# Pair operands in steps, early products, modulation and norm statistics on another engine, in a two-block transformer kernel

## The chip, the cores and the metric

The kernel runs on one core of a Trainium2 chip, as one program. The metric is the device time of one execution in microseconds; of several runs the median is taken. In the profile the engines are PE (TensorE, matrix products), DVE (VectorE), ACT (ScalarE), POOL (GpSimd) and SP (SyncE, which issues most transfers).

## What is computed

Two blocks of two layers each, on 1024 tokens of 1024 features, in float32 (products are done as three partial products of a high and a low part).

```python
# first block, per layer
h = x * (1 + scale) + shift              # "modulation": scale, shift, gate from c @ w_mod
u = h @ w_in                             # also for 256 context tokens
y = concat(rwkv(u), attention(u), neighbourhood(u)) * silu(gates)
x = layer_norm(ALPHA * x + gate * (y @ w_out), ln_g, ln_b)
...
# second block
h = layer_norm(x, ln_in_g, ln_in_b)
for l in range(2):
    fq, fk, fv, flog, sq, sk, sv, cq, ckv, krot, mq, gate = split(h @ w_in[l])
    fox = causal_softmax(fq, fk, fv, 1/8, cumsum(log_sigmoid(flog + b)))
    sb  = stick_breaking(sq, sk, sv, 1/8)
    mla = causal_softmax(up(cq), up(ckv) + rope(krot), ..., 96 ** -0.5)
    mem = softmax(mq @ mk / 8) @ mv      # 256 memory tokens
    h = layer_norm(ALPHA * h + (concat(fox, sb, mla, mem) * silu(gate)) @ w_out[l], ln_g[l], ln_b[l])
```

## The kernel before, in words

The input of a layer is kept transposed in SBUF as a high and a low half, `hthi` and `htlo`, in groups of tokens `GROUPS = ((0, 256), (256, 512), (768, 512))`: the context, and two halves of the 1024 tokens. From the second block on there is no group 0. A projection of 128 columns for one group is 24 matmuls (`proj_part`, `proj_b`): eight chunks of features, three partial products each. `open_layer` makes room for the next layer's halves and loads and splits its first 128 columns of weights.

**Between layers.** `out_proj` works on tiles of 128 tokens: 48 matmuls into two tiles `po`; in the first block a multiply by the gate (`r`, L1713); `x = ALPHA x + r` (L1715); `layer_norm`, in the last layer of the first block a second one with the second block's first weights (`post`); the store; and `put_ht`, which turns the tile (`xtp`, L109), in the first block's first layer modulates it (`hmod`, L409, eight instructions of 128 columns per tile on DVE with two per-partition operands), and splits it into `hthi` (ACT, L127) and `htlo` (DVE, L128). `layer_norm` takes its statistics with `bn_stats` on DVE (L183, L184), the inverse root by ACT and DVE, then 384 columns on ACT, POOL and DVE and 640 on DVE. `out_proj` is not in a fixed order: the framework orders each engine's instructions by a simulated time line. The next layer's first projection (`conv(..., 9)` in `project`, or `bcols` of `ckv` in `block2_layer`) follows in PSUM tiles `pj`, whose pool is opened after `out_proj` has closed its own.

**Attention of the second block.** Within `self.ordered()` PE executes in the order of the program text; the other engines are ordered by the framework. Two streams of steps are woven by `seqs`: `soft_heads` (two pairs of MLA heads, two pairs of fox heads) at rate 48 and `other_heads` (two pairs of stick-breaking heads, two pairs of memory heads) at rate 32. The stream whose count of steps, each of 1/rate, is lowest goes next. A pair begins with `pump(todo, 0)`, which executes the transposes and products that the pair before still owes, then makes its operands: `queries2` (load, scaled copy on ACT, copy to the other half by POOL, low part on DVE, per head: `bform`, L1204 and L1208), `keys2` (load, two casts on ACT, two low parts on DVE: `aform`, L1194 to L1197), `values2` (a load). `spare` gives the room of the raw load: for the soft stream the tag "P" (two buffers, also the room of the weights), for the other stream the one buffer "sa" of the stick-breaking weights. Then come two yields (`gap`: at a stream's first pair with `GAP` = 3 fillers each), and the pair's units: eight tiles of queries, 12 steps in a causal pair, four steps in a memory pair.

A step issues scores for one group (`weigh`), then what is due of the groups before (`turn`: transposes of the weights `PTp` and their copies `PT`; after every four blocks `fill`, one filler; `blend`: the product with the values, `Yp`). The filler generator gives pieces of the layer's other projections, six matmuls each (`proj2`), then the split of the output weights. `need` draws fillers until the named projections are done.

```python
seqs((self.soft_heads(ap, proj), 48), (self.other_heads(ap, proj, l), 32))
...
Q = self.queries2(pool, "a", 6 + p, scale)
K = self.keys2(pool, "a", 4 + p)
V = self.values2(pool, "a", 4 + p)
...
self.need(proj, ("g", 4 + p))
yield from self.gap(p == 0)
yield from self.causal(pool, todo, "a", 4 + p, ...)
```

The functions that the change touches:

Of the kernel before, what the change touches and what calls it, by code (L numbers as in the profile page):

```python
# [71 lines left out]
class Kern:  # L72
    def __init__(self, tc, A, out):
# [12 lines left out]
        self.ptp = None  # L86

# [89 lines left out]
    def layer_norm(self, pool, src, dst, g, b):  # L177

        nc = self.nc
        st = self.tl(pool, [128, 2, 6], F32, "lnst", 2)  # L180
        mv = self.tl(pool, [128, 5], F32, "lnmv", 2)
        for i in range(2):
            nc.vector.bn_stats(st[:, i, :], src[:, i * 512:(i + 1) * 512])  # L183
        nc.vector.bn_aggr(mv[:, 0:2], st)  # L184
        self.rstd(mv[:, 2:3], mv[:, 1:2], 1.0, 1e-5, mv[:, 3:4], mv[:, 4:5])
# [206 lines left out]
    def put_ht(self, sp, pp, ht, t, xt, mc):  # L392
# [5 lines left out]
        for half in range(2):  # L398
# [85 lines left out]
    def project(self, l, ht, full, first, fp, sd, att):  # L484
# [4 lines left out]
        with ExitStack() as es:  # L489
# [109 lines left out]
    def conv(self, sp, pp, ht, hi, lo, j, bufs=5):  # L599
# [5 lines left out]
        for g, (s, n) in enumerate(GROUPS):  # L605
            ps = yield from self.psteps(pp, ht, g, hi, lo)
# [592 lines left out]
    def bform(self, B, L, raw, scale, side=(0, 1)):  # L1199

        nc = self.nc
        for h in range(2):
# [476 lines left out]
    def out_proj(self, es, wo, tiles, t0, l, g, b, gated, mc, xi, xo, post=None, side=None):  # L1679
# [4 lines left out]
        sp = self.pool(es, "op", side=side)  # L1684
        pp = self.pool(es, "opp", space=PSUM, side="right")
# [11 lines left out]
        for t in tiles:  # L1697
# [6 lines left out]
            for c in range(2):  # L1704
# [55 lines left out]
    def block2_layer(self, l, i):  # L1760
# [8 lines left out]
        with ExitStack() as es:  # L1769
# [4 lines left out]
            with ExitStack() as s3:  # L1774
                mp = self.pool(s3, "mla", side=far)
                up = self.pool(s3, "up2", space=PSUM)
# [7 lines left out]
                self.bcols(pj, ht, *first, 0, 128, ckv)  # L1784
                for hi, lo, m, dst in self.ahead(fp, st, W, ((1, 36, kf), (2, 128, cq[:, 0]), (3, 128, cq[:, 1]))):
                    self.bcols(pj, ht, hi, lo, 0, m, dst)
# [61 lines left out]
    def bcols(self, pp, ht, hi, lo, c0, m, dst):  # L1848
        for g in (1, 2):
            s, n = GROUPS[g]  # L1850
            ps = self.proj_b(pp, ht, g, hi, lo, c0, m)
# [186 lines left out]
    def keys2(self, pool, tag, j):  # L2038
        K = self.tl(pool, [128, 2, NL], F32R, tag + "K")
        raw = self.spare(pool, tag)  # L2040
        self.load(raw, self.RK[j])
# [19 lines left out]
    def soft_heads(self, pool, proj):  # L2061
# [6 lines left out]
        kf = self.spare(pool, "a")  # L2068
# [5 lines left out]
        for p in range(2):  # L2074
            self.pump(todo, 0)
            Q = self.queries2(pool, "a", 6 + p, scale)
            K = self.keys2(pool, "a", 4 + p)
            V = self.values2(pool, "a", 4 + p)
            raw = self.spare(pool, "a")
            self.load(raw, self.QP)  # L2080
# [8 lines left out]
            yield from self.gap(p == 0)  # L2089
            yield from self.causal(pool, todo, "a", 4 + p, lambda h, t, tk, n: self.qk_scores(  # L2090
                Q, h, K[:, h], tk, self.span(n), t, extra=(qr[:, h], krs)), V)
        for p in range(2):
            self.need(proj, ("q", p), ("k", p), ("v", p), ("g", p))
            self.pump(todo, 0)
            Q = self.queries2(pool, "a", p, 0.125)
            K = self.keys2(pool, "a", p)
# [4 lines left out]
            yield  # L2101
            yield
# [185 lines left out]
```

## Time and profile before

| | us |
|---|---|
| median of three runs | 3996.33 |
| the three runs | 3978.35, 3996.33, 4007.02 |
| the profiled execution | 3984.52 |
| its span, first to last instruction | 3982.7 |
| PE busy in it | 3608.7 |
| DVE, ACT, POOL busy | 2639.5, 1713.5, 1166.4 |

Mean granted clock of TensorE: 0.955 of full speed; it has two levels, 1.2 and 2.4 GHz. In a row of the timeline stand the start, the duration, the engine, the line, the operation, the tiles (out<-in), the shapes, the count, and in brackets the idle time of the engine before it and what ended it. PE's rows overlap, as matmuls are pipelined. Stages by their start in the span: first block's first layer 0, its output projection 1183, second layer 1331, its output projection 2367, second block's projections 2497, attention 2655, output projection 3161, second layer's projections 3262, attention 3385, output projection 3885.

### The profile page before, as it was taken

How to read it: one execution, taken by the hardware profiler on the slowest of the kernel's cores; microseconds unless marked ns; L12 is line 12 of the kernel's file. 1: busy time of each engine (PE TensorE's matmuls, PEld its weight loads, DVE VectorE, ACT ScalarE, POOL GpSimd, SP SyncE). 2: the span in 40 equal slices, each digit the busy share in tenths (PEclk: the TensorE clock that was granted, in tenths of full speed). 3: DMA queues.
4: the chain of work that ended last, by engine and by line, in shares of the span. 5: the costliest groups of instructions: out<-in, count | busy, mean ns of one | idle time of the engine just before them, and what ended most of it. 6: DMA issues, size and time to landing. Idle time of an engine off the chain costs nothing. (4 is left out here: it accounts for less than half of the span.)

```text
span 3982.7 us, 67431 instructions
## 1 busy us (share of the span) xinstructions
PE 3608.7 (91%) x25828; PEld 2696.0 (68%) x25828; DVE 2639.5 (66%) x4778; ACT 1713.5 (43%) x3352; POOL 1166.4 (29%) x1175
## 2 busy tenths in 40 slices
PE   7999998989979899898999888999889899888988
PEld 5767776666537777676666546677667677666767
DVE  4546886677878745886686769556665554676654
ACT  3236553444442335553444342345454423555451
POOL 2200012556662210001566653031111311221232
PEclk8999998999989999898999999999999999999999
DMA  7437864242533227875243522341222332322233
GB/s 252 162 116 185 200 164 144 87 137 87 177 106 106 83 77 182 185 186 167 84 136 97 173 90 90 127 137 64 80 83 83 130 122 95 103 83 86 87 98 130
DMA packets 509843, 495.74 MB, mean 124 GB/s; under 512 B 296360, under 2 KB 412616, under 8 KB 505168
## 3 DMA queue, kind: packets, MB, share of 16 engines
q1 hardware_dynamic: 469264, 455.76, 38.2%
q10 hardware_dynamic: 40256, 35.66, 3.0%
q8 instruction: 204, 3.34, 0.4%
q14 instruction: 119, 0.97, 0.1%
HBM read 323.81 MB, written 167.49 MB: 123 GB/s over the span
## 5 line engine op out<-in xcount | busy, mean ns | idle before, releaser
L106 PE MATMUL pj<-hthi,hhi 128*128 128x512 f32 (+2 forms) x2120 | 857.2, 404 | 22.9 <-DVE stg L712 13.1
L106 PE MATMUL pj<-hthi,hlo 128*128 128x512 f32 (+2 forms) x2120 | 805.4, 380 | 0.0
L106 PE MATMUL pj<-htlo,hhi 128*128 128x512 f32 (+2 forms) x2120 | 804.5, 379 | 0.4 <-DVE htlo L128 0.4
L106 PEld LDWEIGHTS pj<-hthi,hhi 128*128 128x128 f32 (+1 forms) x2120 | 407.3, 192 | 126.8 <-issue 23.6
L106 PEld LDWEIGHTS pj<-hthi,hlo 128*128 128x128 f32 (+1 forms) x2120 | 405.5, 191 | 79.6 <-DVE hlo L128 0.4
L106 PEld LDWEIGHTS pj<-htlo,hhi 128*128 128x128 f32 (+1 forms) x2120 | 408.6, 193 | 61.0 <-DVE htlo L128 1.6
L1554 POOL TENSOR_TENSOR acc<-acc,gP 128x512 f32<-128x512 f32 (+1 forms) x240 | 306.4, 1291 | 140.0 <-ACT gP L1548 123.5
L1548 ACT ACTIVATE gP<-T 128x512 f32<-128x512 f32 (+1 forms) x292 | 166.9, 582 | 167.3 <-PE T L106 153.8
L1460 DVE TENSOR_REDUCE gmx<-S 128x1 f32<-128x512 f32 (+1 forms) x372 | 202.1, 554 | 47.1 <-PE S L106 44.9
L106 PE MATMUL po<-who,yh 128*128 128x512 f32 x544 | 214.6, 395 | 11.0 <-ACT yh L1668 8.5
L127 ACT CAST hhi<-hraw 128x1024 fp32r<-128x1024 f32 x118 | 123.8, 1049 | 231.2 <-PE pj L106 194.3
L106 PE MATMUL po<-wlo,yh 128*128 128x512 f32 x544 | 214.3, 394 | 0.0
L106 PE MATMUL po<-who,yl 128*128 128x512 f32 x544 | 212.1, 392 | 0.7 <-POOL yl L1669 0.7
L106 PE MATMUL S<-K,B 128*128 128x512 f32 (+2 forms) x448 | 168.9, 381 | 46.3 <-DVE gmx L1460 34.7
L106 PE MATMUL Y<-gP,V 128*64 128x512 f32 (+1 forms) x776 | 203.2, 603 | 3.0 <-DVE ys L1567 2.9
L128 DVE TENSOR_TENSOR hlo<-hraw,hhi 128x1024 fp32r<-128x1024 f32 x84 | 102.8, 1223 | 128.3 <-ACT hhi L127 127.4
L106 PE MATMUL T<-B,K 128*128 128x512 f32 (+1 forms) x368 | 167.9, 457 | 10.5 <-ACT gP L1548 9.2
L1189 POOL TENSOR_SCALAR RL<-rl 128x128 f32<-128x128 f32 (+1 forms) x80 | 34.6, 434 | 469.6 <-DVE rl L1306 417.8
L106 PEld LDWEIGHTS S<-K,B 128*128 128x128 f32 x448 | 86.6, 193 | 122.3 <-DVE gmx L1460 73.7
L128 POOL TENSOR_TENSOR hlo<-hraw,hhi 128x1024 fp32r<-128x1024 f32 x34 | 87.0, 2559 | 256.4 <-ACT hhi L127 249.6
L106 PE MATMUL S<-KL,L 128*128 128x512 f32 (+2 forms) x448 | 153.7, 353 | 2.0 <-ACT KL L1380 2.0
L106 PE MATMUL T<-L,KL 128*128 128x512 f32 (+1 forms) x368 | 144.7, 394 | 0.0
(420 smaller groups left out, 8037.3 us busy)
## 6 DMA issues: line engine op xcount, KB each, us to landing
hraw<-in_w_in_dram SPq DMA_DIRECT2D x110, 512.0 KB
T<-d_PRE SPq DMA_DIRECT2D x40, 768.0 KB
mw<-in_w_mod_dram SPq DMA_DIRECT2D x24, 1024.0 KB
RKK<-d_U SPq DMA_DIRECT2D x80, 288.0 KB
yl<-d_YT ACTq DMA_DIRECT2D x34, 512.0 KB
d_G<-stg SPq DMA_DIRECT2D x64, 256.0 KB
woraw<-in_w_out_dram SPq DMA_DIRECT2D x32, 512.0 KB
d_PRE<-T SPq DMA_DIRECT2D x40, 384.0 KB
```

What stands on the lines that cost most here:

```text
L106: self.nc.tensor.matmul(out, lhsT=lhsT, rhs=rhs, start=start, stop=stop, skip_group_check=True)
L127: self.nc.scalar.copy(hi, src)
L128: self.lo_engine.tensor_tensor(out=lo, in0=src, in1=hi.bitcast(F32), op=ALU.subtract)
L1189: self.nc.gpsimd.tensor_scalar(out=out, in0=in_, scalar1=1.0, scalar2=0.0, op0=ALU.mult, op1=ALU.add)
L1460: nc.vector.tensor_reduce(out=m, in_=S[:, 0:w], op=ALU.max, axis=AX.X, negate=True)
L1548: nc.scalar.activation(P, T, AF.Exp)
L1554: eng.tensor_tensor(out=acc[h][:, cs], in0=acc[h][:, cs], in1=P, op=ALU.add)
```

## The change

Five things are changed.

1. Operands of a pair (second block). `gap` becomes `step`, one yield, with three fillers before it if it is told that it is the stream's first. `spare` also issues the load; query and key loads of a pair are issued together, in "P" (soft stream) or in two of the three buffers "sc" (other stream). `queries2` yields after each head, and there is a step after the loads and one after the keys: four per pair; in a memory pair three.
2. Early products. In `out_proj`, after the matmuls of the last tile and before its norm, the first 128 columns of the next layer are multiplied for groups 0 and 1, where they exist, into PSUM tiles of their own (`early`). `conv` and `bcols` take them instead of making them.
3. Modulation in `put_ht` goes from DVE to ACT (the first block's first layer, 80 instructions; 16 more for the memory tokens).
4. Sums. In the norm `post`, for all but the last two tiles, mean and variance come from two ACT passes with `accum_out` instead of `bn_stats`.
5. The pool `up2` is opened after the first `bcols`.

```diff
-    def layer_norm(self, pool, src, dst, g, b):
+    def layer_norm(self, pool, src, dst, g, b, sums=False):
...
+        if sums:
+            junk = self.tl(pool, [128, D], BF16, "lnj")
+            nc.scalar.activation(junk, src, AF.Identity, scale=-1.0 / D, accum_out=mv[:, 5:6])
+            nc.scalar.activation(junk, src, AF.Square, bias=mv[:, 5:6], accum_out=mv[:, 1:2])
+            nc.vector.tensor_scalar(out=mv[:, 0:1], in0=mv[:, 5:6], scalar1=-1.0, scalar2=None, op0=ALU.mult)
...
-                    nc.vector.tensor_scalar(out=h[:, j, :], in0=ps[:, j, :], scalar1=mc[:, v, 8 + k:9 + k],
-                                            scalar2=mc[:, v, k:k + 1], op0=ALU.mult, op1=ALU.add)
+                    nc.scalar.activation(h[:, j, :], ps[:, j, :], AF.Identity, scale=mc[:, v, 8 + k:9 + k], bias=mc[:, v, k:k + 1])
...
                 dd = self.drain(self.conv(kq, pp, ht, *first, 9))
+                self.early[0].close()
...
-            ps = yield from self.psteps(pp, ht, g, hi, lo)
+            ps = self.early[1].pop(g, None)
+            if ps is None:
+                ps = yield from self.psteps(pp, ht, g, hi, lo)
...
+        groups = [g for g in (0, 1) if nht and g in nht]
+        if nht:
+            ep = self.pool(self.early[0], "early", space=PSUM, side="right" if 0 in nht else "left")
...
+            if t == tiles[-1]:
+                for g in groups:
+                    n = GROUPS[g][1]
+                    ps = self.early[1][g] = self.tl(ep, [128, 512], F32, f"early{g}")[:, :n]
+                    self.proj_part(ps, nht, g, *self.nht[2], 0, 8)
             self.layer_norm(sp, x, x, gr, br)
             if post:
-                self.layer_norm(sp, x, x, pg, pb)
+                self.layer_norm(sp, x, x, pg, pb, sums=t < tiles[-2])
...
-    def gap(self, first):
-
-        for _ in range(2):
-            for _ in range(GAP if first else 0):
-                next(self.filler, None)
-            yield
+    def step(self, first=False):
+
+        for _ in range(GAP if first else 0):
+            next(self.filler, None)
+        yield
...
-    def spare(self, pool, tag):
-
-        return self.tl(pool, [128, NL], F32, "P", 2) if tag == "a" else self.tl(pool, [128, NL], F32, "sa")
-
-    def queries2(self, pool, tag, j, scale):
+    def spare(self, pool, tag, src):
+
+        raw = self.tl(pool, [128, NL], F32, *(("P", 2) if tag == "a" else ("sc", 3)))
+        self.load(raw, src)
+        return raw
+
+    def queries2(self, pool, tag, raw, scale, first=False):
...
-        raw = self.spare(pool, tag)
-        self.load(raw, self.RQ[j])
-        self.bform(B, L, raw, scale)
+        for h in range(2):
+            self.bform(B, L, raw, scale, heads=(h,))
+            yield from self.step(first)
         return B, L
...
         for p in range(2):
             self.pump(todo, 0)
-            Q = self.queries2(pool, "a", 6 + p, scale)
-            K = self.keys2(pool, "a", 4 + p)
+            rq, rk = self.spare(pool, "a", self.RQ[6 + p]), self.spare(pool, "a", self.RK[4 + p])
             V = self.values2(pool, "a", 4 + p)
-            raw = self.spare(pool, "a")
-            self.load(raw, self.QP)
+            yield from self.step(p == 0)
+            Q = yield from self.queries2(pool, "a", rq, scale, p == 0)
+            raw = self.spare(pool, "a", self.QP)
+            K = self.keys2(pool, "a", rk)
+            yield from self.step()
...
             self.need(proj, ("g", 4 + p))
-            yield from self.gap(p == 0)
             yield from self.causal(pool, todo, "a", 4 + p, lambda h, t, tk, n: self.qk_scores(
...
-            Q = self.queries2(pool, "b", 2 + p, 0.125)
-            K = self.keys2(pool, "b", 2 + p)
+            rq, rk = self.spare(pool, "b", self.RQ[2 + p]), self.spare(pool, "b", self.RK[2 + p])
             V = self.values2(pool, "b", 2 + p)
-            yield from self.gap(p == 0)
+            yield from self.step(p == 0)
+            Q = yield from self.queries2(pool, "b", rq, 0.125, p == 0)
+            K = self.keys2(pool, "b", rk)
+            yield from self.step()
```

The fox pairs (soft stream) and the memory pairs (other stream) are changed alike, without fillers in their steps.

## Rows read from the trace of the kernel before

**Rows 1.** The page, first part: busy time, share of the span, instructions.

```profile
PE 3608.7 (91%) x25828; PEld 2696.0 (68%) x25828; DVE 2639.5 (66%) x4778; ACT 1713.5 (43%) x3352; POOL 1166.4 (29%) x1175
```

**Rows 2.** Windows, stages: length, then busy (instructions) PE, PEld, DVE, ACT, POOL; clock, DMA.

```profile
1183.00:1331.00 148.00, 123.49 (x559) 99.74 (x559) 117.92 (x245) 34.04 (x61) 34.90 (x32) 0.93 0.35 110
...
2367.00:2497.00 130.00, 106.64 (x468) 84.96 (x467) 108.23 (x228) 34.73 (x73) 43.15 (x28) 0.91 0.28 93
...
2655.00:3161.00 506.00, 441.57 (x2901) 340.80 (x2899) 327.82 (x488) 268.44 (x480) 121.56 (x88) 0.95 0.27 88
3161.00:3262.00 101.00, 99.10 (x465) 82.40 (x466) 58.76 (x121) 23.52 (x46) 25.07 (x16) 1.00 0.43 144
```

**Rows 3.** Windows, twelve pair changes (position 1.0, sum); then the rest of both stages.

```profile
3040.00:3070.00 30.00, 26.61 (x171) 21.73 (x170) 17.59 (x29) 16.07 (x32) 10.51 (x6) 0.89 0.41 132
...
3765.00:3795.00 30.00, 25.17 (x154) 20.39 (x150) 16.77 (x27) 16.32 (x32) 10.50 (x6) 0.89 0.42 132
...
sum 300.00, PE 232.22 PEld 181.92 DVE 217.25 ACT 174.57 POOL 122.79; mean PE 19.35 PEld 15.16 DVE 18.10 ACT 14.55 POOL 10.23
...
sum 706.00, PE 645.43 PEld 495.27 DVE 436.76 ACT 362.71 POOL 116.59; mean PE 53.79 PEld 41.27 DVE 36.40 ACT 30.23 POOL 9.72
```

**Rows 4.** Timeline, MLA's second pair to fox's first pair, first layer.

```profile
2902.93 0.88 SPq L113 DMA_DIRECT2D P<-d_RQ  x1
...
2905.82 0.32 SPq L113 DMA_DIRECT2D P<-d_RK  x1
...
2912.47 1.62 DVE L1195 TENSOR_TENSOR aK<-P,aK 64x1024 fp32r<-64x1024 f32 x1
...
2914.24 0.30 PE L106 MATMUL S<-aK,aB 128*128 128x128 f32 x1 [3.76 <-DVE aK L1195]
...
2916.95 0.44 PE L106 MATMUL S<-aK,aB 128*128 128x128 f32 x1 [2.23 <-DVE aK L1197]
```

**Rows 5.** Waits of PE, whole span: us in total, times, longest us.

```profile
PE PTp L109 <- ACT sc L1348: 6.2, 2, 4.9
```

**Rows 6.** Timeline of PE, then of DVE, end of the first output projection.

```profile
1301.99 1.09 PE L109 MATMUL xtp<-CST,x 128*128 128x128 f32 x8 [2.54 <-DVE x L198]
...
1325.22 1.97 PE L109 MATMUL xtp<-CST,x 128*128 128x128 f32 x8 [9.57 <-DVE x L198]
...
1341.20 0.39 PE L106 MATMUL pj<-hthi,hhi 128*128 128x512 f32 x1
...
1329.22 1.37 DVE L409 TENSOR_SCALAR hmod<-xtp,MODC 128x128 f32<-128x128 f32 x4
...
1336.98 0.69 DVE L128 TENSOR_TENSOR htlo<-hmod,hthi 128x512 fp32r<-128x512 f32 x1 [0.69 <-ACT hthi L127]
```

**Rows 7.** Timeline of PE, end of the second output projection.

```profile
2474.73 0.79 PE L106 MATMUL pj<-hthi,hhi 128*128 128x512 f32 x1 [5.12 <-DVE r L1713]
...
2488.99 1.94 PE L109 MATMUL xtp<-CST,x 128*128 128x128 f32 x8 [7.00 <-issue]
2496.63 1.94 PE L109 MATMUL xtp<-CST,x 128*128 128x128 f32 x8 [5.70 <-issue]
```

**Rows 8.** Groups by shape: L409, L189, L138 first output projection; L183 second.

```profile
L409 DVE TENSOR_SCALAR hmod<-xtp,MODC 128x128 f32<-128x128 f32 x80 | 27.3, 402 | 0.8
...
L189 ACT ACTIVATE x<-x,lnmv 128x384 f32<-128x384 f32 x10 | 7.1, 710 | 27.7 <-DVE lnmv L186 27.7
...
L138 ACT ACTIVATE lnmv<-lnmv 128x1 f32<-128x1 f32 x10 | 2.0, 202 | 8.7 <-DVE lnmv L132 8.6
...
L183 DVE BATCH_NORM_STATS2 lnst<-x 128x6 f32<-128x512 f32 x32 | 21.4, 688 | 0.6
```

**Rows 9.** Groups by shape, ACT, first attention stage.

```profile
L1267 ACT ACTIVATION_READ_ACCUMULATOR P<-S,mx 128x1 f32 x64 | 12.8, 200 | 0.0
...
L1341 ACT ACTIVATE sa<-sa 128x1024 f32<-128x1024 f32 x6 | 6.4, 1061 | 0.2
```

**Rows 10.** Chain that ended last, at position 1.0, first layer: start, us, what.

```profile
3042.11 7.04 PE pj L106 x30
```

More of the change, by code (lines that the diff above doesn't have):

```diff
@@ L86, in __init__ @@
         self.ptp = None
+        self.early = ExitStack(), {}
     def nm(self, s):
@@ L175, in whalf @@
         return hi, lo
-    def layer_norm(self, pool, src, dst, g, b):
+    def layer_norm(self, pool, src, dst, g, b, sums=False):
         nc = self.nc
[L180 to L185, printed above, removed]
+        mv = self.tl(pool, [128, 6], F32, "lnmv", 2)
+        if sums:
[3 more added lines that the diff above has]
+            nc.vector.tensor_scalar(out=mv[:, 0:1], in0=mv[:, 5:6], scalar1=-1.0, scalar2=None, op0=ALU.mult)
+        else:
+            st = self.tl(pool, [128, 2, 6], F32, "lnst", 2)
+            for i in range(2):
+                nc.vector.bn_stats(st[:, i, :], src[:, i * 512:(i + 1) * 512])
+            nc.vector.bn_aggr(mv[:, 0:2], st)
+        self.rstd(mv[:, 2:3], mv[:, 1:2], 1.0 / D if sums else 1.0, 1e-5, mv[:, 3:4], mv[:, 4:5])
         nc.vector.scalar_tensor_tensor(out=mv[:, 3:4], in0=mv[:, 0:1], scalar=-1.0, in1=mv[:, 2:3], op0=ALU.mult, op1=ALU.mult)
@@ L1197, in aform, with bform @@
         nc.vector.tensor_tensor(out=a1[0:64], in0=src[64:128], in1=a1[64:128].bitcast(F32), op=ALU.subtract)
-    def bform(self, B, L, raw, scale, side=(0, 1)):
+    def bform(self, B, L, raw, scale, side=(0, 1), heads=(0, 1)):
         nc = self.nc
-        for h in range(2):
+        for h in heads:
             r, o = slice(64 * h, 64 * h + 64), slice(64 - 64 * h, 128 - 64 * h)
@@ L1850, in bcols @@
             s, n = GROUPS[g]
-            ps = self.proj_b(pp, ht, g, hi, lo, c0, m)
+            ps = self.early[1].pop(g, None)
+            if ps is None:
+                ps = self.proj_b(pp, ht, g, hi, lo, c0, m)
             self.copy(dst[:, s - NCX:s - NCX + n], ps)
@@ L2032, in queries2, with keys2 @@
         L = self.lows[tag]
-        raw = self.spare(pool, tag)
-        self.load(raw, self.RQ[j])
-        self.bform(B, L, raw, scale)
+        for h in range(2):
+            self.bform(B, L, raw, scale, heads=(h,))
+            yield from self.step(first)
         return B, L
-    def keys2(self, pool, tag, j):
+    def keys2(self, pool, tag, raw):
         K = self.tl(pool, [128, 2, NL], F32R, tag + "K")
-        raw = self.spare(pool, tag)
-        self.load(raw, self.RK[j])
         self.aform(K[:, 0], K[:, 1], raw)
@@ L2100, in soft_heads @@
                 self.load(nf[:, h], self.NF[2 * p + h].unsqueeze(0).to_broadcast([128, NL]))
-            yield
-            yield
+            yield from self.step()
+            Q = yield from self.queries2(pool, "a", rq, 0.125)
+            K = self.keys2(pool, "a", rk)
+            yield from self.step()
             yield from self.causal(pool, todo, "a", p, lambda h, t, tk, n: self.qk_scores(
@@ L2112, in other_heads @@
             self.pump(todo, 0)
-            Q = self.queries2(pool, "b", 2 + p, 0.125)
-            K = self.keys2(pool, "b", 2 + p)
+            rq, rk = self.spare(pool, "b", self.RQ[2 + p]), self.spare(pool, "b", self.RK[2 + p])
             V = self.values2(pool, "b", 2 + p)
-            yield from self.gap(p == 0)
+            yield from self.step(p == 0)
+            Q = yield from self.queries2(pool, "b", rq, 0.125, p == 0)
+            K = self.keys2(pool, "b", rk)
+            yield from self.step()
             yield from self.causal(pool, todo, "b", 2 + p, lambda h, t, tk, n: self.qk_scores(
@@ L2124, in other_heads @@
             self.pump(todo, 0)
-            mk = self.spare(pool, "b")[:, 0:256]
+            rq = self.spare(pool, "b", self.RQ[4 + p])
+            mk = self.tl(pool, [128, NL], F32, "sc", 3)[:, 0:256]
             self.load(mk, self.MK[l, p])
+            yield from self.step()
             ma = self.tl(pool, [128, 2, NL], F32R, "bK")
             self.aform(ma[:, 0, 0:256], ma[:, 1, 0:256], mk)
-            Q = self.queries2(pool, "b", 4 + p, 0.125)
+            Q = yield from self.queries2(pool, "b", rq, 0.125)
             at, done = self.frames(pool, todo, "b", 6 + p)
-            yield
-            yield
             for t in range(0, 8, 2):
```

8 lines of the change are left out of this document (4 added, 4 removed).

## The prediction

> **What bounds the kernel now.** I read the page's first part first: PE is busy 91% of the span, no other engine over 66% [rows 1]. So time can only come from PE's idle stretches, or from those in which it works at the lower of its two clock levels. Then the windows, one per stage [rows 2]: the first output projection leaves PE 148.00 - 123.49 = 24.5 us idle, the second 23.4, the first attention stage of the second block 64.4; the reader is to see that the granted clock (0.93, 0.91, 0.95) is low there too, while the third output projection, 99.10 of 101.00, has nothing to give.
>
> Then the windows of both attention stages, cut where a stream goes from one pair of heads to the next: six places per layer, twelve in all, 300 us, and the 706 us between them [rows 3]. PE is idle in 300.00 - 232.22 = 67.8 us of the twelve, 23%; in the rest in 60.6 us, 9%. If the twelve were like the rest they would be idle 26 us: 42 are theirs alone. The timeline of one [rows 4] shows the serial chain: query load issued at 2902.93, key load at 2905.82, the key's low part on DVE at 2912.47, and PE, which has nothing else ahead in its fixed order, stands 3.76 us and then 2.23 us for the two heads. From load to first score 11.3 us. The waits show the other stream suffering there as well: transposes held up to 4.9 us for stick-breaking weights [rows 5].
>
> Last the timelines between layers. After the first output projection PE waits 9.57 us for the last but one tile's x, does its transposes, and only then the first products for tokens it has had for long; the product of the last 512 tokens begins at 1341.20 [rows 6]. After the second one PE does a product at 2474.73 in the middle of the waiting and then stands 7.00 and 5.70 us for x [rows 7].
>
> **The change part by part.** *Early products, first to second layer.* The product of the first 256 and the next 512 tokens (24 matmuls each) moves ahead of the last tile's norm. At full clock that is 8.4 us: 24 of 512 columns at 7.04/30 us [rows 10] and 24 of half the width. The 9.57 us stall holds them. What is late next is the low half of the last tile, ready at 1336.98 + 0.69 = 1337.7 [rows 6]. So alone the move gives 1341.2 - 1337.7 = 3.5 us.
>
> *Modulation.* 80 instructions go from DVE to ACT: 27.3 us of DVE busy time [rows 8], in a stage where DVE is busy 117.92 of 148 us and ACT 34.04 [rows 2]. The price on ACT is not in the trace; bounds are an ACT instruction of one column, 0.202, and one of 384 columns with a scale and a bias per partition, 0.710 [rows 8]. 128 columns lie nearer the lower end: I take 0.4, four of them 1.6 against 1.37 on DVE [rows 6]. The last tiles' halves are then no quicker each (1.6 + 0.62 cast + 0.69 against 1.37 + the same), but the DVE queue before them is shorter by four such groups, 5.4 us, and the first x comes up to that much earlier: I take 4, and 2.5 from the DVE stall inside the stage, at 1301.99 [rows 6]. Together 3.5 + 4 + 2.5 = 10 us; ends 3 (ACT at 0.71 each, no shorter queue) and 15.
>
> The Trainium skill, "ScalarE: Activation LUTs", section Rules for kernel authors, speaks against this edit: adds and multiplies belong on VectorE. By the cost the page measures (186 ns, 93 more for each of two per-partition operands, 0.833 per column, 93 saved back to back) four instructions are an estimated 1.64 us, and the rule would charge the last four halves about 1 us of the 10. The rows show why it need not decide here: DVE is the full queue, ACT the empty one [rows 2].
>
> *Sums.* In the second output projection the statistics of the second norm move to ACT for six of eight tiles. DVE loses 6 x 2 x 0.67 = 8.0 us [rows 8], the aggregation besides, and gets one one-column instruction a tile back: 8 us off 108.23 busy of 130 [rows 2]. ACT gets 6 x 2 passes over 1024 columns at 1.06 and an accumulator read at 0.200 each [rows 9]: 15 us, on an engine busy 34.73 of 130. Each such tile's chain grows by 2 x 1.26 - 1.4 = 1.1 us, covered by the next tile's matmuls; if it were not, 6 x 1.1 = 7 us. DVE being the fuller queue and the waits lying at its end [rows 7], what it is relieved of arrives there; but the last two tiles don't use it. I take 6 us; ends 0 and 12.
>
> *Early products, the two later boundaries.* Nothing: at the first of these the product already sits in the wait [rows 7]; it moves from 2474.73 to some 2465, and x is as late as before. At the next PE is idle 1.9 us in the whole stage [rows 2]. Cost if the cover fails: 5.6 us.
>
> *Operands in steps.* No instruction is added. Both loads are issued at once, in rooms that no longer pass through the one stick-breaking buffer; each head's query, then the key, is followed by a step. Four steps per pair replace two (three in the memory pairs), so by the streams' rates (48 and 32) the other stream gets 4 x 32/48 = 2.7 of its own steps into PE's order instead of 1.3 while the soft stream's 11.3 us chain runs, and DVE and ACT see the other stream's work between operand pieces instead of behind all of them. A step of the other stream carries a score group, a turn with one or two projection pieces of 6 matmuls (1.4 us each) and sometimes a blend, about 5 us: 13 us, over the 11.3. SP gets the same loads earlier, POOL the same copies. At a layer's start 18 projection pieces instead of 12 are put between the operands.
>
> One place per layer cannot gain: fox's second pair and the first memory pair both start at position 1.0 (soft step 48 at rate 48, other step 32 at rate 32; before 42/48 and 28/32, also equal). There both streams are empty. Today 30 projection matmuls, 7.04 us, pulled in by the need for a gate, cover it [rows 10]; with six pieces spent earlier there is less or nothing to pull. I book +2 us a layer, up to +7.
>
> For the other ten places: idle 67.8 less (30.00 - 26.61) and (30.00 - 25.17) is 59.6 us in 240, 21 of it the ordinary 9%: 39 are to be had [rows 3]. 60% of it, 23 us, because the key's load waits for the pair before to be transposed, as now. The lower clock goes along: a clock of 0.95 over 506 us is 25 us of lost full speed a layer [rows 2], part of it while idle; I give 8 in all to the ten places. Sum 23 + 8 - 4 = 27 us for both layers; ends -10 (the other stream's chain holds PE as well) and 55 (all 42, and 13 of clock).
>
> **Sum.** 10 + 6 + 0 + 27 = 43 us off the profiled execution's 3984.5 (span 3982.7, 1.8 around it): 3941.5. That execution lies 11.8 below the median of the three runs, 3996.33; the same 43 off the median gives 3953.
>
> **The rivals.** *A: attention gives nothing.* PE's order then holds other-stream units whose weights aren't ready, and the stall only changes its name to transposes behind sc, as in the 4.9 us wait [rows 5]. For it: that wait stands beside an operand chain already today. Against: DVE no longer does whole operands ahead of that stream. Time 3996 - 16 = 3980.
>
> *B: everything goes.* All 42 us, 13 of clock, and the upper half of the boundaries, 23: 78 us, 3918. For it: 13 us of cover against 11.3. Against: the shared position 1.0.
>
> *C: slower.* The six pieces spent at a layer's start are missed at position 1.0: with 7.04 us of cover gone and both streams empty, the chain from the key's load to the first score, 2914.24 - 2905.82 = 8.4 us [rows 4], stands bare, and 4 us of lower clock behind it: 25 us in two layers. With it A's mechanism, 3 us at each of the ten other places, since two more yields leave PE to a stream that isn't ready: 30. Less 16 from the boundaries: 3996 + 39 = 4035. It decides once the other stream needs more than 11.3 us for 2.7 steps. Against: where idle is largest that stream is full of projections.
>
> **How the numbers follow.** Forecast 0.55, with its own range 3935 to 3973; A 0.20; B 0.17; C 0.08. One per cent, 40 us, is about what a measurement of this kernel can tell from no change, and the line is 3956: 0.6 of the forecast lies below it, 0.33, with all of B 0.50 faster. Same: the rest of the forecast 0.22, A 0.20, part of C 0.03: 0.45. Slower 0.05. The range 3908 to 3994 leaves out C, the far end of B and the weak end of A.
>
> **What would show it.** Right: the second layer's product of the last 512 tokens begins some 10 us earlier after the matmuls of the output projection; no hmod on DVE; the twelve places idle near 45 us, PE's waits on aK gone; ACT's accumulator reads in the second output projection, and PE's two waits there near 8 us instead of 12.7. Wrong: waits of transposes on sc grow by what waits on aK lose (A); PE stands over 8 us where fox's second pair begins (C); the third boundary, or the first block's scan, moves by more than 5 us, which nothing here foresees.

## The result: slower by half a per cent, and the profile after

The changed kernel takes 4008.32 us (median of 20 runs) against 3988.56 us for the kernel before beside it: ratio 1.0054, 95% interval 1.004 to 1.0068, 20 us slower. The profiled execution of the changed kernel spans 4024.3 us, some 18 above its own median.

Aligning the two profiles by the same matmul in each shows where the 42 us between the spans arise. Up to the end of the first output projection and the projections behind it the changed kernel gains 19 us. A stretch of the first block, at 1475, then loses 17; it shows in profiles of unchanged first blocks too (last section). The rest of the first block and the second output projection lose 12, the projections before attention gain 4. The two attention stages of the second block lose 19.1 and 17.2 us: that is the loss to be explained.

The page of the changed kernel, answering to [rows 1]:

```profile
PE 3635.7 (90%) x25828; PEld 2714.8 (67%) x25828; DVE 2614.6 (65%) x4670; ACT 1758.3 (44%) x3472; POOL 1159.5 (29%) x1175
```

Its windows for the first and second output projection and the first attention stage, answering to [rows 2]:

```profile
1183.00:1325.00 142.00, 133.66 (x623) 110.64 (x624) 101.39 (x174) 61.05 (x142) 35.52 (x32) 0.96 0.35 115
2377.00:2511.00 134.00, 105.19 (x459) 83.89 (x458) 101.33 (x216) 49.74 (x99) 37.00 (x26) 0.87 0.30 98
2646.00:3186.00 540.00, 465.66 (x2973) 359.04 (x2971) 337.29 (x494) 272.35 (x487) 121.94 (x93) 0.93 0.26 87
```

The window of the kernel before for the same stretch of the first attention stage:

```profile
2640.00:3161.00 521.00, 455.17 (x2973) 352.03 (x2972) 334.42 (x494) 273.42 (x487) 129.40 (x93) 0.95 0.28 90
```

The stage holds the same 2973 matmuls and is 19 us longer. PE is idle 74.3 us of it against 65.8, and busy 10.5 us longer with the same work, as the granted clock is 0.93 of full speed against 0.95. So a little under half is waiting, the rest the clock. Both attention stages of the changed kernel together:

```profile
sum 1057.00, PE 907.65 PEld 699.19 DVE 664.06 ACT 540.08 POOL 240.83; mean PE 453.82 PEld 349.60 DVE 332.03 ACT 270.04 POOL 120.42
```

The kernel before has 1021.00 and 891.25. Of the 36 us between them 19.6 are idle time of PE (149.4 against 129.8), and 16.4 are time in which it is busy.

The waits of PE in the kernel before, whole span, for the key's low part:

```profile
PE S L106 <- DVE aK L1195: 12.9, 4, 3.8
PE S L106 <- DVE aK L1197: 6.3, 4, 2.2
```

The same view of the changed kernel, with what PE waits for instead:

```profile
PE PTp L110 <- ACT sc L1357: 26.0, 8, 5.3
PE Yp L107 <- DVE PT L122: 16.3, 17, 3.5
PE Yp L107 <- ACT PT L124: 14.9, 12, 3.8
PE S L107 <- DVE aK L1204: 5.4, 2, 2.9
PE S L107 <- DVE aK L1206: 2.2, 2, 1.1
```

Of what the change was to remove, more than half is removed: 12.9 + 6.3 us of waiting for the key are 5.4 + 2.2. Transposes waiting for stick-breaking weights, 6.2 us in [rows 5], are 26.0. One place shows how. This is the timeline of the change from MLA's second pair to fox's first, the place of [rows 4]: PE, then DVE, then ACT.

```profile
2922.23 1.09 PE L107 MATMUL Yp<-PT,aV 128*64 128x128 f32 x14 [0.23 <-ACT PT L124]
2923.33 0.42 PE L107 MATMUL S<-bK,bB 128*128 128x384 f32 x1
...
2929.57 0.44 PE L107 MATMUL Yp<-PT,bV 128*64 128x128 f32 x4 [3.49 <-DVE PT L122]
2932.52 0.50 PE L107 MATMUL S<-bK,bB 128*128 128x512 f32 x1
...
2940.00 1.12 PE L110 MATMUL PTp<-CST,sc 128*128 128x128 f32 x4 [5.33 <-ACT sc L1357]
2949.07 0.66 PE L110 MATMUL PTp<-CST,sc 128*128 128x128 f32 x4 [2.27 <-ACT sc L1357]
2953.91 0.33 PE L107 MATMUL S<-aK,aB 128*128 128x128 f32 x1
...
2926.17 1.22 DVE L1204 TENSOR_TENSOR aK<-P,aK 64x1024 fp32r<-64x1024 f32 x1
2928.23 0.95 DVE L1348 COPY sc<-S 128x768 f32<-128x768 f32 x1
2929.54 1.22 DVE L1206 TENSOR_TENSOR aK<-P,aK 64x1024 fp32r<-64x1024 f32 x1
2938.12 0.95 DVE L1356 TENSOR_TENSOR sc<-sc,sa 128x768 f32<-128x768 f32 x1
...
2918.91 2.14 ACT L1213 ACTIVATE aB<-P 64x1024 fp32r<-64x1024 f32 x2 [0.24 <-DMA P<-d_RQ]
2939.11 0.84 ACT L1357 ACTIVATE sc<-sc 128x768 f32<-128x768 f32 x1 [4.38 <-DVE sc L1356]
```

The key's second low part is done at 2929.54 + 1.22 = 2930.76. Fox's first score begins at 2953.91, 23 us later, without a wait: its turn had not come. Between the stick-breaking scores behind MLA's last product (2923.33) and it lie 30.6 us in which PE's order holds stick-breaking units and projection pieces only, with waits of 3.49, 5.33 and 2.27 us, 11.1 in all. The same stretch in the kernel before (timeline of PE) goes from 2909.09 to fox's first score at 2914.24 [rows 4] and is 5.2 us long:

```profile
2909.09 0.48 PE L106 MATMUL S<-bK,bB 128*128 128x512 f32 x1
...
2929.54 1.11 PE L109 MATMUL PTp<-CST,sc 128*128 128x128 f32 x4 [4.87 <-ACT sc L1348]
```

The scores issued at 2923.33 have their weights at 2939.11 + 0.84 = 2939.95, 16.6 us later, through DVE and ACT, and the steps left in between don't fill that. The operands wait for PE now, not PE for the operands. ACT's row shows the second thing: both heads' scaled copies still stand back to back (x2), as DVE and ACT are ordered by the framework's simulated time, not by the text. So they do at all 16 pairs of both stages, as in the kernel before. The steps reach PE's order alone.

This place shows how the waits change, not that they grow. Before, PE waits 3.76 and 2.23 us for the key and, right behind, 4.87 for the weights, 10.9 in all, and now 11.1. They grow over all twelve places. Windows of 43 us, each from 3 us before a pair's query load, kernel before:

```profile
sum 516.00, PE 434.97 PEld 339.88 DVE 346.25 ACT 286.84 POOL 181.67; mean PE 36.25 PEld 28.32 DVE 28.85 ACT 23.90 POOL 15.14
```

The changed kernel:

```profile
sum 516.00, PE 416.02 PEld 322.24 DVE 337.07 ACT 271.51 POOL 146.90; mean PE 34.67 PEld 26.85 DVE 28.09 ACT 22.63 POOL 12.24
```

Idle PE goes from 81.0 to 100.0 us, nearly all of the 19.6. Half of that, 9.1 to 18.9, lies in the two windows of the first memory pair, at position 1.0.

The Trainium skill, "TensorE: Matmul & The Clock Gate", section "Step-by-step: what each phase is for", states that matmuls stay in program order and only weight loads are pulled ahead. This trace agrees: fox's scores, whose operands were ready, did not go before the transposes at 2940.00 in their 5.33 us.

### The profile page after: what moved, and what is told of

Its sections match the earlier page's. It is cut to its first block, busy times and chain, and to the rows that moved or that the text cites. A ratio compares the mean times of both kernels' runs of the same rounds, so it can differ in the third digit from the quotient of the medians.

```text
span 4024.3 us, 67454 instructions
## 1 busy us (share of the span) xinstructions
PE 3635.7 (90%) x25828; PEld 2714.8 (67%) x25828; DVE 2614.6 (65%) x4670; ACT 1758.3 (44%) x3472; POOL 1159.5 (29%) x1175
## 4 chain that ended last, share of the span: by engine, by line
PE 65%; DVE 15%; issue 6%; ACT 6%; DMA 6%; POOL 1%; SPq 1%; ACTq 0%; DVEq 0%; POOLq 0%
PE pj L107 27%; PE S L107 6%; PE po L107 6%; PE rw L107 5%; PE T L107 4%; PE Y L107 3%; PE pre L107 3%; PE Yp L107 2%; PE PTp L110 2%; PE msc L107 1%; SPq L114 1%; DVE sa L1354 1%; DMA yl<-d_YT 1%; PE up L107 1%; PE msc L110 1%
## 5 line engine op out<-in xcount | busy, mean ns | idle before, releaser
L110 PE MATMUL PTp<-CST,P 128*128 128x128 f32 x704 | 116.1, 287 | 36.2 <-DVE PT L122 25.2
```

Source lines behind the costliest of these rows:

```text
L110: self.nc.tensor.transpose(out, in_, ident)
```

## The experiments

Each is timed against the kernel before on the same chip. "Attention" is what the two attention stages of the second block lose in the profile, by the same matmuls (the change: 36).

**The change in two halves, its rooms alone, and without the sums.** The parts between the layers alone (e1) and the operand part alone (e2), each against the change:

```diff
-            yield from self.step(p == 0)
-            Q = yield from self.queries2(pool, "a", rq, scale, p == 0)
+            Q = self.queries2(pool, "a", 6 + p, scale)
...
+            yield from self.gap(p == 0)
```

```diff
-                    self.proj_part(ps, nht, g, *self.nht[2], 0, 8)
...
-                self.layer_norm(sp, x, x, pg, pb, sums=t < tiles[-2])
+                self.layer_norm(sp, x, x, pg, pb)
```

> Only the parts between the layers (early products, modulation on ACT, sums on ACT); operands as before. Theory 1 (the operand steps cost the time, the parts between layers pay): 15 us faster than before, some 3973 against 3988; the attention stages as before, 479 and 474 us from first score to first output projection. Theory 2 (the parts between the layers cost it, by the longer chain of the sums and a lower clock after the early products): 10 us or more slower than before.

> Only the operand part (steps, rooms, fillers at a layer's start); everything between layers as before. Theory 1: 30 to 35 us slower than before, near 4020; PE's waits for sc and for the copies PT in the two attention stages grow by some 20 us a layer, its waits for aK fall from 9 to 4. Theory 2: within 5 us of before or faster.

e1: 3981.46 us, 0.9973 (0.9953 to 0.9994); attention 4. e2: 4025.59 us, 1.0075 (1.005 to 1.0099); attention 39. About 11 us gained and 30 lost give the 20 of the change: the whole loss lies in the operand part.

Rooms and early loads of the change, whole operands, then the two old yields (e3); and early products with modulation, no sums (e4):

```diff
             Q = yield from self.queries2(pool, "a", rq, scale, p == 0)
...
-            yield from self.step()
+            yield from self.gap(p == 0)
```

> Of the operand part only the loads: query and key loads together and in rooms of their own; the whole operands are made before the two old yields, with the old 12 fillers, so the order on PE is that of before. Theory 1 (PE's order costs it): within 8 us of before. Rival (the rooms cost it: the weights' buffers P and sc are held by raw loads, and the loads come at another time on SP): half or more of what e2_steps loses, 15 us or more slower.

> As e1_between without the sums on ACT (the norms keep bn_stats on DVE). If the sums' longer chain holds PE in the second output projection, as the 4 us longer stage there suggests: 4 to 6 us faster than e1_between. If DVE's relief pays as predicted: 6 us slower than e1_between.

e3: 3995.86 us, 1.0005 (0.9983 to 1.0028): loads and rooms cost and bring nothing. e4: 3987.18 us, 0.9975 (0.9953 to 0.9996), as much as with the sums.

**Fillers, place or number of the steps.** The operand part with 12 fillers, not 18 (e5); four steps behind whole operands (e6); two steps in the change's places (e7):

```diff
-GAP, ALF, LAG, LAGS, PACE = 3, 32, 1, 2, 1.0
+GAP, ALF, LAG, LAGS, PACE = 2, 32, 1, 2, 1.0
```

```diff
-    def gap(self, first):
+    def gap(self, first, n=4):
 
-        for _ in range(2):
+        for i in range(n):
```

```diff
         for h in range(2):
             self.bform(B, L, raw, scale, heads=(h,))
-            yield from self.step(first)
+            if h == 0:
+                yield from self.step(first)
...
-            yield from self.step()
```

> Operand part alone as in the run of the operand part (25 to 31 us over the kernel before there), with two fillers per step in each stream's first pair, so 12 of them as before, not 18. Theory 1, the count of steps: four yields per pair (three in the memory pairs) in place of two let PE's written order take a run of the other stream's units whose weights are not ready, at every pair; the fillers are only work moved ahead. Then nearly all of the loss stays: 4015 to 4030 us, and the long waits of PE's transposes on sc stay. Theory 2, the fillers: the six pieces spent early are missing later. Then at least half of the loss goes: 3995 to 4010 us. Theory 3, placement (the key's operands and the first score come later because the steps stand between the pieces): the fillers are part of what stands between, so a little comes back, 4010 to 4025 us.

> The loads in rooms of their own and the whole operands first, as in the run with the rooms alone (no difference there), but then four yields (three in the memory pairs) in place of the two; 12 fillers. The count of steps is that of the operand part, their place is behind the operands. Theory 1, the count: as the operand part alone, 4015 to 4030 us. Theory 3, the place: as the rooms alone, 3990 to 4002 us.

> The loads in rooms of their own and the steps in the places of the change, but only two per pair: after the loads, and after the first head's query; 12 fillers. The count is that of the kernel before, the place that of the change. Theory 1, the count: as the rooms alone, 3990 to 4002 us. Theory 3, the place: 4008 to 4025 us, since the key's operands stand behind two of the steps as before they stood behind none.

e5: 4040.96 us, 1.0119 (1.0095 to 1.0143), attention 49. The six added fillers are not the cause: without them the loss is, if anything, larger than e2's. e6: 4031.49 us, 1.0095 (1.0071 to 1.0119), attention 45. e7: 3996.18 us, 1.0009 (0.9991 to 1.0027), attention 8. So the place is free and the number costs: two steps in either place lose nothing measurable, four in either lose 30 to 50 us. The timeline of e6 (PE, then DVE) is that of the change again, though its operands are made in one go:

```profile
2926.31 0.42 PE L106 MATMUL S<-bK,bB 128*128 128x384 f32 x1
...
2940.60 1.12 PE L109 MATMUL PTp<-CST,sc 128*128 128x128 f32 x4 [4.72 <-ACT sc L1348]
...
2952.09 1.06 PE L109 MATMUL PTp<-CST,sc 128*128 128x128 f32 x4 [4.83 <-ACT sc L1348]
...
2958.51 0.33 PE L106 MATMUL S<-aK,aB 128*128 128x128 f32 x1
...
2930.93 1.22 DVE L1197 TENSOR_TENSOR aK<-P,aK 64x1024 fp32r<-64x1024 f32 x1
```

The key is ready at 2932.15, the score comes at 2958.51. In e7 PE waits for the key at the same place, as in the kernel before (timeline of PE):

```profile
2928.73 0.32 PE L106 MATMUL S<-aK,aB 128*128 128x128 f32 x1 [3.98 <-DVE aK L1195]
...
2931.44 0.45 PE L106 MATMUL S<-aK,aB 128*128 128x128 f32 x1 [2.04 <-DVE aK L1197]
```

**Which stream's steps.** On e6: four steps in the soft stream alone (f1), in the other alone (f2), one step everywhere (f3):

```diff
-            yield from self.gap(p == 0)
+            yield from self.gap(p == 0, 2)
```

in `other_heads` for f1, in `soft_heads` for f2, and for f3 with 1 in both:

> Rooms and whole operands first, as in the two runs before; four steps behind them in the soft stream's pairs only (MLA, fox), two in the other stream's. Four in both cost 38 us (ratio 1.0095). Theory 1a: during the soft stream's four steps PE's order holds only stick-breaking or memory units, and a stick-breaking unit's weights come through seven instructions of DVE and ACT, so PE waits for sc; the loss sits in this half: 4010 to 4027 us against 3990. Theory 1b: either stream alone is too slow, each half costs the same: 4003 to 4012 us here and in the next run. Theory 3 (only the total ratio of the streams' lengths matters, four against four being neutral): the waits on sc would not grow.

> The other half: two steps behind the operands in the soft stream's pairs, four in the stick-breaking pairs, three in the memory pairs. Theory 1a: while the other stream pauses PE's order holds softmax units, whose chain to the weights is short (a maximum and an exponential): 3988 to 4002 us. Theory 1b: 4003 to 4012 us, as in the run before.

> One step behind the operands in every pair of both streams, the 12 fillers of the first pairs as before. If the count is a balance (too few: PE stands for the key's operands; too many: PE stands for the weights of the stream that is alone), this is on the other side of it: waits on aK grow by some 3 us a place, 12 places, waits on sc vanish: 3995 to 4030 us. If fewer steps are simply better: 3960 to 3985 us.

f1: 4055.89 us, 1.0149 (1.0126 to 1.0172), attention 64. f2: 4059.55 us, 1.0165 (1.0143 to 1.0187), attention 68. Both lose nearly twice what four in both lose, so neither theory of halves held, nor the view that only the stick-breaking stretches cost. f3: 4029.43 us, 1.0086 (1.0059 to 1.0113), attention 34. One step is no better than four, but not by the key, as this run's waits of PE (whole span) show: 15.9 us beside the 12.9 of the kernel before, not 36 more, and 2.8 beside 6.3 for the second head.

```profile
PE S L106 <- DVE aK L1195: 15.9, 4, 5.4
PE PTp L109 <- ACT P L1272: 11.7, 5, 3.1
PE PTp L109 <- ACT sc L1348: 10.3, 2, 5.2
```

f1 and f2 also end their streams at other times than the kernel before (64/48 against 40/32 steps by rate, and 56/48 against 46/32; before, 56/48 against 40/32). The next two bring the ends back by the rate:

```diff
-                seqs((self.soft_heads(ap, proj), 48), (self.other_heads(ap, proj, l), 32))
+                seqs((self.soft_heads(ap, proj), 55), (self.other_heads(ap, proj, l), 32))
```

and in g2 48 and 37:

> Four steps behind the operands in the soft stream's pairs, two in the other's (65 us lost at rate 48), now at rate 55, so that both streams end where they end in the kernel before (64/55 = 1.16 against 56/48 = 1.17). Pauses alone (half of those of the run with four in both, which lost 38 us): 4005 to 4013 us. If the unequal ends cost nothing and the lone stick-breaking stretches everything: 4040 to 4060 us as at rate 48. If the ends were all: 3988 to 4000 us.

> The other half likewise: four steps (three in memory pairs) in the other stream only, its rate 37 in place of 32 (46/37 = 1.24 against 40/32 = 1.25). Pauses alone: 4005 to 4013 us. If the softmax stream alone costs nothing and the 69 us at rate 32 came from the streams' unequal ends: 3988 to 4000 us. If the ends cost nothing: 4045 to 4065 us.

g1: 4033.71 us, 1.0104 (1.0072 to 1.0137). g2: 4026.0 us, 1.0081 (1.0053 to 1.0109). The rates give back about 25 us (65 to 40) and 37 (69 to 32). That it is the ends isn't shown, as a rate changes the weave of the whole stage. In f2's profile the last product of the soft stream lies 39 us before the end of each attention stage, with 12 us of idle PE behind it, in the kernel before 14 to 15 us with 4 to 6, so there the ends have a part. In f1's the stream that is left alone has 16 us with 4, no more than before. The other 40 and 32 are left, each as large as four steps in both; half of that was expected. Pauses cost, but don't add up.

**The chain to the weights.** The kernel before (g3) and e6 (g4), both without the exponential, the logarithm and the running sum in the stick-breaking weights:

```diff
-        nc.scalar.activation(a, a, AF.Exp, scale=-1.0)
-        nc.scalar.activation(a, a, AF.Ln, bias=1.0)
...
-        for i in range(m):
-            nc.vector.tensor_tensor_scan(out=a[:, i, ::-1], data0=self.ones.to_broadcast([128, n]), data1=a[:, i, ::-1],
-                                         initial=0.0, op0=ALU.mult, op1=ALU.add)
```

> The kernel before with the chain from a stick-breaking score to its weights shortened: the exponential, the logarithm and the running sum are left out of it (two ACT passes and the DVE scans of each unit). It is there for the difference to the next run. By itself: PE's work is unchanged, a lighter ACT and DVE: 3955 to 3990 us.

> Four steps behind whole operands in both streams (38 us lost with the full chain), with the same parts of the stick-breaking chain left out as in the run before. If PE's wait for the weights of the stream that is alone makes the loss, the difference to the run before falls to 0 to 15 us. If it is anything else in the order (transposes waiting for their copies, the lower clock, pairs ending late), the difference stays 28 to 45 us.

g3: 3947.31 us, 0.9887 (0.9856 to 0.9918). g4: 3966.88 us, 0.9935 (0.9914 to 0.9957). The difference is 20 us where it was 38. The windows of both attention stages together (length, then busy), in e6; the kernel before has 1021.00 and 891.25:

```profile
sum 1066.00, PE 907.32 PEld 697.00 DVE 666.03 ACT 538.12 POOL 246.42; mean PE 453.66 PEld 348.50 DVE 333.02 ACT 269.06 POOL 123.21
```

The same in g3:

```profile
sum 981.00, PE 885.71 PEld 687.16 DVE 566.54 ACT 468.22 POOL 236.07; mean PE 442.85 PEld 343.58 DVE 283.27 ACT 234.11 POOL 118.04
```

And in g4:

```profile
sum 988.00, PE 879.67 PEld 679.69 DVE 577.55 ACT 465.18 POOL 238.65; mean PE 439.84 PEld 339.85 DVE 288.78 ACT 232.59 POOL 119.33
```

With the full chain two more steps per pair lengthen the stages by 45 us, with the short one by 7. PE's wait for sc in g4 is 1.4 us in all, in e6 23.5. But the 7 flatter: PE's idle time grows by 13.0 us (95.3 to 108.3), while PE is busy 6.0 us less for nearly the same matmuls (5824 in the windows against 5835), at a clock of 0.97 in both stages against 0.96 and 0.95. With the full chain idle time grows by 28.9 (129.8 to 158.7). So the chain to the weights is somewhat over half of the waiting, and half of the loss by the times; what makes the rest isn't shown. The edit also takes work off ACT and DVE (DVE 666 us to 578), so a shorter chain and lighter engines aren't told apart. Ahead of attention g4's profile has the low-clock stretch of the last section (18.6 us), which g3's has not; how far that enters the times isn't known.

**Other work at the changes, another rate.** On e1: projections kept for the pair changes (f4), and the soft stream's rate 44 (e8); then e4 at that rate (h2):

```diff
-GAP, ALF, LAG, LAGS, PACE = 3, 32, 1, 2, 1.0
+GAP, ALF, LAG, LAGS, PACE = 3, 32, 1, 2, 0.85
...
-            yield from self.gap(p == 0)
+            yield from self.gap(True)
```

```diff
-                seqs((self.soft_heads(ap, proj), 48), (self.other_heads(ap, proj, l), 32))
+                seqs((self.soft_heads(ap, proj), 44), (self.other_heads(ap, proj, l), 32))
```

> The parts between the layers alone (3981 against 3995 in their run), the operands of the kernel before, and the layer's other projections kept for the pair changes: pace 0.85 in place of 1 within the pairs, six fillers behind the operands of both MLA pairs and both stick-breaking pairs, not of the first alone. If what a pair change lacks is work that needs no weights, 3965 to 3978 us. If the projections are needed within the pairs just as much: 3980 to 3995 us.

> The parts between the layers alone (about 11 us under the kernel before in their own run), the operands as in the kernel before, and the soft stream's rate 44 in place of 48, so that fox's second pair and the first memory pair no longer begin at the same position. If two streams empty at once is what costs idle time there, 3970 us; if the weave was matched to the readiness of the weights as it stands, 3985 to 4000 us.

> Early products and modulation alone (0.9975 in their own run), no sums, the operands of the kernel before, the soft stream's rate 44. The sums cost some 4 us in the second output projection of the profiles that have them: without them 2 to 4 us under the run with rate 44 and sums (0.9984), so a ratio of 0.997 to 0.9975. If the sums are worth nothing either way in the time: 0.998 to 0.9985.

f4: 4017.71 us, 1.0063 (1.0041 to 1.0085), slower than either expectation. That within the pairs the projections were covering waits too would fit; it wasn't traced. e8: 3983.18 us, 0.9984 (0.9966 to 1.0001); h2: 3982.61 us, 0.9983 (0.9968 to 0.9997). The rate of 44 brings nothing, and with or without the sums the time is the same.

**The change with two steps, without the sums** (h1: e7's edit on the change, and the old statistics):

```diff
-            yield from self.step(first)
+            if h == 0:
+                yield from self.step(first)
...
-                self.layer_norm(sp, x, x, pg, pb, sums=t < tiles[-2])
+                self.layer_norm(sp, x, x, pg, pb)
```

> The change with two of its four steps per pair (after the loads and after the first head's query; 12 fillers) and without the sums: early products, modulation and rooms as in the change. If the two steps too many are the whole of what the change loses, the gain between the layers is left: 3975 to 3985 us against 3991 before. If the operand part in this place still costs with the early products in front of it: 3990 to 4005 us.

3978.48 us, 0.9966 (0.9952 to 0.998), attention 1: faster than both kernels, 12 us under the one before beside it. With the two further steps per pair gone the loss is gone.

## Why the prediction was wrong

Forecast 3953 us, result 4008, outside the range. The step that failed is *operands in steps*, booked at -27 us; alone it costs 30 (e2). It had 23 us of PE's idle time and 8 of lower clock come back. In the changed kernel's attention stages idle time grows by 19.6 us, and PE is busy 16.4 longer, at a lower clock (0.93 against 0.95 in the first stage). Its premises one by one:

- *"about 5 us: 13 us, over the 11.3"*: two more yields did put more of the other stream in front of the soft scores, but that took 30.6 us at the place of [rows 4], not 13: 19.5 of work and 11.1 of waits. A step was priced by its matmuls, and these too low. Alone in PE's order, its units stand for their own chain, 16.6 us from score to weights, and PE then works at the lower clock (four transposes take 1.12 us at 2940.00, 0.66 at 2949.07).
- *"DVE and ACT see the other stream's work between operand pieces"*: they do not, as the x2 on ACT shows. e7 agrees: the place of the steps is worth nothing.
- A bare key at position 1.0 (C's first half) did not come: PE's longest wait for a key in the changed kernel is 2.9 us, not 8, and fewer fillers at the start (e5) made it no better. C's second half and A's mechanism, PE left to a stream whose weights aren't ready, did. The 4.9 us wait of [rows 5] was its sign. I took it for a stall that only changes its name. At the place of [rows 4] it does just that (10.9 us to 11.1); over the twelve places it exceeds what it replaces. That C's 30 us equal e2's loss is luck: C had them at ten places and by waiting alone, while half of the added idle time lies at the other two, position 1.0, and the clock is nearly half of the loss. The sign "idle near 45 us" at the twelve places went the other way, by the windows above.

The other terms:

- *Early products and modulation, -10*: right, about -10 in time (e4; by its interval 2 to 19, so that the close agreement is in part luck). In the profile the first boundary gives 12 to 15 us. The timeline of the change, PE and then ACT:

```profile
1187.30 0.80 PE L107 MATMUL po<-who,yh 128*128 128x512 f32 x1 [8.34 <-ACT yh L1677]
...
1319.62 0.50 PE L107 MATMUL pj<-hthi,hhi 128*128 128x512 f32 x1 [1.86 <-ACT hthi L128]
...
1303.13 1.51 ACT L416 ACTIVATE hmod<-xtp,MODC 128x128 f32<-128x128 f32 x4 [0.66 <-DVE htlo L129]
```

The start of that output projection in the kernel before (timeline of PE):

```profile
1191.18 0.79 PE L106 MATMUL po<-who,yh 128*128 128x512 f32 x1 [7.90 <-ACT yh L1668]
```

  The product of the last 512 tokens begins 132.3 us after the stage does, against 150.0 [rows 6]. Four modulations on ACT take 1.51 us, 1.6 assumed. The estimate of 1.64 us from the Trainium skill, "ScalarE: Activation LUTs", section What ACT_TABLE_LOAD costs, is near that. Its rule (section Rules for kernel authors) to keep such work on VectorE agrees with the price of the instruction (1.37 us on DVE). Whether following it would have been the better choice isn't shown. No run has the early products without the modulation, so the 3.5 us booked for the one and the 6.5 for the other aren't told apart.
- *Sums, -6*: wrong. DVE is relieved (108.23 us busy to 101.33), ACT pays 15.4 us against 15 foreseen, and the stage gets no shorter. PE's wait at its end, for x through the last two tiles that keep the old statistics, is 19.02 us with the sums and 16.99 without (e4), the early product being done before it in both. The timeline of PE in the change:

```profile
2499.16 1.94 PE L110 MATMUL xtp<-CST,x 128*128 128x128 f32 x8 [19.02 <-issue]
```

Its groups by shape on ACT in that stage:

```profile
L185 ACT ACTIVATE lnj<-x,lnmv 128x1024 bf16<-128x1024 f32 x6 | 6.9, 1150 | 0.2
L184 ACT ACTIVATE lnj<-x 128x1024 bf16<-128x1024 f32 x6 | 6.3, 1058 | 10.9 <-DVE x L205 10.9
...
L185 ACT ACTIVATION_READ_ACCUMULATOR lnj<-x,lnmv 128x1 f32 x6 | 1.1, 187 | 0.0
L184 ACT ACTIVATION_READ_ACCUMULATOR lnj<-x 128x1 f32 x6 | 1.1, 186 | 0.0
```

The timeline of PE in e4:

```profile
2484.52 1.94 PE L110 MATMUL xtp<-CST,x 128*128 128x128 f32 x8 [16.99 <-issue]
```

  I said that relief of the fuller queue "arrives there". The queue got shorter and the wait at the end did not, so it isn't the queue; I take it for one tile's chain, which wasn't traced. In time the sums show no difference (e1 and e4, e8 and h2).
- *Early products at the later boundaries, 0*: the projections behind the second one are 3 to 4 us shorter in all profiles that have the early products, the third boundary 0 to 2 us; neither was traced further.

What stays open: why one step per pair loses 34 us without one wait that carries it, why four steps in one stream at matched ends cost as much as four in both, and what makes the half of the loss that the shorter chain leaves. The order of units that two steps give fits the chains better than its neighbours on either side; no run shows a rule for it beyond the wait for the lone stream's weights.

## What to carry to other kernels

A yield between two streams of hand-ordered matmuls is not a place where work is hidden for free: it hands PE to the other stream, and that stream alone is worth only what its own chain from score to weights allows. Fewer yields aren't better by themselves: one per pair lost as much as four (f3). Price such a step by that chain, not by its matmuls, and look whether the engines that make the operands follow the same order at all. Before moving work off a full queue, see whether the wait to be shortened is the queue or one tile's chain.

## What was not expected of the hardware

In the changed kernel's profile TensorE runs at the lower of its two levels, 1.2 GHz, for some 37 us in the first block, while it is busy throughout. The windows of the changed kernel:

```profile
1475.00:1510.00 35.00, 35.00 (x77) 20.00 (x76) 8.79 (x11) 3.64 (x5) 1.14 (x2) 0.50 0.27 93
1510.00:1530.00 20.00, 20.00 (x113) 15.98 (x111) 10.52 (x25) 11.88 (x30) 0.40 (x2) 0.96 0.58 135
```

The window of the kernel before:

```profile
1475.00:1510.00 35.00, 34.20 (x145) 21.74 (x145) 18.95 (x20) 9.29 (x12) 2.09 (x3) 1.00 0.30 109
```

What PE did before the clock fell (timeline of the changed kernel): one wait of 0.80 us.

```profile
1470.15 0.39 PE L107 MATMUL pj<-hthi,hlo 128*128 128x512 f32 x1
1471.34 1.12 PE L107 MATMUL msc<-k,CST 2*128 2x512 f32 x2 [0.80 <-DVE k L144]
...
1475.98 0.80 PE L107 MATMUL pj<-hthi,hhi 128*128 128x512 f32 x1
```

The kernel before has the same wait at full clock. The stretch costs 17 to 19 us and shows in the profiles of f3, f4, g1, g4 and h1 too (for a part of it in four more), whether or not the first block was touched; the ten others, the kernel before among them, have none of it. In five of the six the profiled execution lies 10 to 25 us above its kernel's median, so it seems to belong to an execution; with one profile of each kernel that isn't shown. The Trainium skill, "TensorE: Matmul & The Clock Gate", section "Seeing it yourself", warns that clock records can be unreliable and that the gate was seen stuck low for over 50 us; here the matmuls themselves are slower (77 in 35 us, not 145), so it is the clock and not the record. What sets it off no run shows.
